# Seven products instead of eight in the second MLP product, with weight sums made in HBM

## The chip, the cores and the metric

The kernel runs on one core of a Trainium2 chip. The core has a matrix engine (TensorE, in the profile PE, with its weight loads as PEld), a vector engine (VectorE, DVE), a scalar engine (ScalarE, ACT), a general engine (GpSimd, POOL) and a queue that only issues transfers and waits (SyncE, SP). Each works through a queue of its own in order; they wait for each other by semaphores. Transfers are issued from SP, ACT or POOL and carried out by 16 DMA engines. The metric is the device time of one execution in microseconds.

## What is computed

One layer of a hybrid decoder on 512 tokens of 1024 channels, all in float32. What matters here is its last part, a squared-ReLU MLP with 4096 hidden channels:

```
x = x + mixed @ w_out
h = rms_norm(x, norm_mlp)
x = x + square(relu(h @ w_ff1)) @ w_ff2
out = rms_norm(x, norm_final)
```

Ahead of it come a causal pooling mixer and a sparse-attention mixer (projections of the normed input, a small MLP that compresses keys and values, rotary embedding, two softmax branches), merged by sigmoid gates. `w_ff1` is 1024 x 4096 and `w_ff2` 4096 x 1024, each 16 MB.

## The kernel before

Every matrix product of float32 numbers is made of three: each operand is split in a high part (a copy in the format that TensorE takes, by ScalarE) and a low part (the rest, by VectorE), and high x high, high x low and low x high are summed in PSUM. So each weight tile of 512 KB (128 x 1024 float32) is loaded to a raw tile, split into a pair of tiles, and then used. `emit_load` issues the loads in the order of a list `LD` on SP as raw tiles come free; `emit_prep_half` splits, in the order of a list `WL`; `use` hands out the split pair. `ahead()` is called between matmuls and prepares a few weights beyond the one in use.

The stages, with their times in the profile of before:

- 0 to 175 us: the input is normed and turned, and all projections with the pooling mixer and the compression run (`P1`, one weight tile of 512 KB after the other, each about 5.6 us of TensorE). Each of the key and query projections goes through `rope`, which copies PSUM out on ACT (L512) and swaps halves by four small DMAs on SP.
- to 395 us: attention, in 96 slots, with the remaining projections filled in between.
- to 476 us: the projection of the attention (`pn`), the output projection (`wo`), the residual sum, the second norm, and its transposition into quarters.
- to 777 us and to the end: the MLP in four chunks of 1024 hidden channels.

In the first MLP product each chunk is two groups of 512 hidden channels, and each group is a product of a 2 x 2 block matrix of weights (four quarters of 512 x 256) with a 2 x 2 block matrix of activations. It is done by seven block products instead of eight (Strassen's algorithm in Winograd's form). The seven are called A11, A12, A22, S1, S2, S3 and S4: the first three use a quarter of the weights as it is, the others use sums. VectorE makes the weight sums in place in the raw tiles (L231 to L238): S1 = 21 + 22, S3 = 11 - 21, S2 = S1 - 11, S4 = 12 - S2. Each block product is 24 matmuls with 256 columns (8 places x 3 products of parts), L1241, accumulated in a bank of PSUM; `Group.main` and `Group.last` combine the banks (L1285 to L1304), and `act` applies relu and square and splits the result into the two tiles `aT`. The second product of a chunk is plain: `tm3` runs 192 matmuls with 512 columns (L320) into eight banks and `add_x` (L1150) adds them to the residual, in both halves of the output channels. Between the two `drain_side()` completes what VectorE and ScalarE still have to do.

Eight raw tiles serve the MLP: four of the ring of the earlier stages and four cut from `oT`, the attention's output, once it is used up. Three pairs of split tiles go round.

The code is written in one order, with generators (`side`) that interleave the side work. The framework then sets the order of each engine's queue by its own planner, which may move an instruction ahead of others that stand before it in the text when its operands are ready and its engine has room in the plan. Transfers issued by SP and ACT are given eight semaphores in turn, and a transfer waits until the one before it on its semaphore has landed.

Of the kernel before, what the change touches and what calls it, by code (L numbers as in the profile page):

```python
# [62 lines left out]
def trunk(ctx: ExitStack, tc: tile.TileContext, A, out):  # L63
# [28 lines left out]
    def add_w(key, ap):  # L92
        WL.append((key, len(LD)))
        LD.append((ap, None))
# [40 lines left out]
    GROUPS = {}  # L135
# [3 lines left out]
    def add_group(c, g):  # L139

        c0 = 1024 * c + 512 * g
        GROUPS[c, g] = {"raw": {}, "at": {}}
        for q in ("11", "21", "22", "12"):
            r0, o = 512 * (int(q[1]) - 1), c0 + 256 * (int(q[0]) - 1)
            GROUPS[c, g]["at"][q] = len(LD)
            LD.append(([(w_f1[r0:r0 + 512, o:o + 256].rearrange("(k p) c -> p k c", p=128), 0)], (c, g, q)))

    for c in range(4):
        for g in range(2):
            add_group(c, g)  # L150
        if c == 0:
            order = [(g, o) for os in FIRST[:1] for o in os for g in range(2)]
            order += [(g, o) for os in FIRST[1:] for g in range(2) for o in os]
        else:
            order = [(g, o) for g in range(2) for o in IN_TURN]
        for g, o in order:
            WL.append((f"{o}{c}{g}", (c, g, o)))
        for h in range(2):
            for i in range(4):
                add_rows(f"f2{c}{h}{i}", w_f2, 1024 * c + 256 * i, 512 * h)  # L160
# [3 lines left out]
    st = {"load": 0, "prep": 0, "use": 0, "kept": 0}  # L164
    spare, slots_hl = [], []

    def emit_load():
# [4 lines left out]
        segs, quarter = LD[i]  # L172
# [3 lines left out]
        if quarter is None and not strassen_on() or st["kept"] < RAW:  # L176
            st["kept"] += strassen_on()
# [9 lines left out]
        if quarter is None:  # L187
            raws[i] = (t, a, b)
        else:
            GROUPS[quarter[:2]]["raw"][quarter[2]] = t  # L190
        return True

    def strassen_on():

        return st["load"] >= GROUPS[0, 0]["at"]["11"]

    def give_back(*tiles):
        spare.extend(tiles)
        while spare and strassen_on() and emit_load():
            pass  # L200

# [3 lines left out]
    def slot_of(i):  # L205

        if not isinstance(WL[i][1], int) or st["kept"]:
            n = len(slots_hl)
            if n < 2:
                slots_hl.append([wp.tile([128, 1024], FR, tag=f"w{e}", bufs=2, name=f"w{e}{i}") for e in "hl"])  # L210
            else:
                slots_hl.append(slots_hl.pop(0))
            return slots_hl[-1]
        return [wp.tile([128, 1024], FR, tag=f"w{e}", bufs=2, name=f"w{e}{i}") for e in "hl"]

    def group_steps(i):

        c, g, o = WL[i][1]
        G = GROUPS[c, g]
        while len(G["raw"]) < 4:  # L220
            assert emit_load()
        r = G["raw"]
        sm = GBf[:, 1024 + 1024 * g:2048 + 1024 * g]
        src = {"A11": r["11"], "A12": r["12"], "A22": r["22"], "S1": sm, "S2": r["11"], "S3": r["21"], "S4": r["12"]}[o]
        h, l = slot_of(i)
        ACT.activation(h, src, AF.Copy)
        yield
        DVE.tensor_tensor(l, src, h.bitcast(F32), op=ALU.subtract)
        if o == "A11":
            yield  # L230
            DVE.tensor_tensor(sm, r["21"], r["22"], op=ALU.add)  # L231
            yield
            DVE.tensor_tensor(r["21"], r["11"], r["21"], op=ALU.subtract)
            yield
            DVE.tensor_tensor(r["11"], sm, r["11"], op=ALU.subtract)
# [3 lines left out]
        G["done"] = G.get("done", "") + o  # L239
        dead = {"S3": "21", "A22": "22", "S4": "12"}.get(o)  # L240
        if o in ("A12", "S2") and "A12" in G["done"] and "S2" in G["done"]:
            dead = "11"
        hls[i] = tuple(x.rearrange("p (a b) -> p a b", a=4) for x in (h, l))
        if dead:
            give_back(r[dead])

    def emit_prep_half():
# [4 lines left out]
        if not isinstance(WL[i][1], int):  # L252
# [33 lines left out]
        if st["load"] > RAW + GROUPS[0, 0]["at"]["11"]:  # L286
# [114 lines left out]
    op = ctx.enter_context(pool("op"))  # L401
# [160 lines left out]
    with ExitStack() as c1:  # L562
# [222 lines left out]
    with ExitStack() as c2:  # L785
# [240 lines left out]
        for i in range(n + LAG + PLAG):  # L1026
# [18 lines left out]
            if 0 <= i - 1 < n:  # L1045
                weight(i - 1)
            if 0 <= t < n:
# [26 lines left out]
    give_back(*(oTf[:, 1024 * i:1024 * i + 1024] for i in range(4)))  # L1074
# [3 lines left out]
    X1 = [p3.tile([128, D], F32, name=f"x1_{t}") for t in range(NT)]  # L1078
    gB = p3.tile([128, D], F32, name="gB1")
# [3 lines left out]
    nc.sync.dma_start(gB, bcast(A["norm_mlp"][0], D))  # L1083
# [11 lines left out]
    def tm3(key, half, aT, post):  # L1095

        ps = [bank() for _ in range(NT)]
        for i in range(4):
            wH, wL = use(f"{key}{half}{i}")
            for t in range(NT):  # L1100
                sl = slice(128 * t, 128 * t + 128)
                prods = []
                for k in range(2):
                    prods += split_products(aT[0][:, 2 * i + k, sl], aT[1][:, 2 * i + k, sl], wH[:, k, :], wL[:, k, :])
# [6 lines left out]
    def tm3_resident(key, half, aT, post, parts=None):  # L1111
# [4 lines left out]
        for t in range(NT):  # L1116
            sl = slice(128 * t, 128 * t + 128)
            n = 256 if parts and t == NT - 1 else 512
            for c in range(0, 512, n):
                ps = bank()[:, 0:n]  # L1120
                prods = []
                for k in range(8):
                    wH, wL = ws[k // 2]
                    prods += split_products(aT[0][:, k, sl], aT[1][:, k, sl], wH[:, k % 2, c:c + n],
                                            wL[:, k % 2, c:c + n])
# [21 lines left out]
    XB = {b: [quarter(f, i) for f in Rf] for i, b in enumerate(("11", "21", "22", "T1"))}  # L1147

# [17 lines left out]
    with ExitStack() as c3:  # L1166
        q3 = c3.enter_context(pool("q3"))
        mT = (q3.tile([128, 8, S], FR, name="mH"), q3.tile([128, 8, S], FR, name="mL"))
        W1 = (q3.tile([128, 8, S], FR, name="W1H"), q3.tile([128, 8, S], FR, name="W1L"))
        keep([f"wo1{i}" for i in range(4)], W1)  # L1170
        ACT.activation(tick, GB[:, 7, 0:1], AF.Sqrt)
# [15 lines left out]
        tm3("wo", 0, mT, post0)  # L1187

        def to_fm(t):
# [21 lines left out]
            for o, d, x, y in (("T1", XT, XQ["12"], XQ["11"]), ("T3", XQ["12"], XQ["22"], XQ["12"]),  # L1211
                               ("T2", XQ["11"], XQ["22"], XT), ("T4", XQ["21"], XQ["21"], XQ["11"])):
                DVE.tensor_tensor(d[:, :, sl], x[:, :, sl], y[:, :, sl], op=ALU.subtract)
# [12 lines left out]
        tm3_resident("wo", 1, mT, post1)  # L1226
# [3 lines left out]
    slots_hl.insert(0, [a4.tile([128, 1024], FR, name=f"w3{e}") for e in "hl"])  # L1230
# [4 lines left out]
    def product(ps, key, x, first):  # L1235

        w, n = use(key), 0
        for f in range(2):
            for k in range(4):
                for u, v in ((0, 0), (0, 1), (1, 0)):  # L1240
                    PE.matmul(ps[:, 256 * f:256 * f + 256], w[u][:, k, 128 * f:128 * f + 128], XB[x][v][:, k, :],  # L1241
                              start=first and n == 0, stop=n == 23, skip_group_check=True)
# [4 lines left out]

    class Group:


        def __init__(self, c, g, aT):
            self.c, self.g, self.aT = c, g, aT
            self.s = pair(GBf, 6 + g)
            self.u2, self.u3, self.c21 = pair(MAf, 6 + g), pair(MAf, g), pair(MAf, 2 + g)
            self.ps, self.done = {}, set()

        def pe(self, o):
            key = f"{o}{self.c}{self.g}"
# [136 lines left out]
```

## Time and profile before

| | |
|---|---|
| time, median of 3 runs | 829.54 us (826.65 to 830.17) |
| the profiled execution | 829.27 us |
| its span, first to last instruction | 827.5 us |
| mean granted TensorE clock | 0.994 |
| PE / PEld busy | 801.9 us (97%) / 695.0 us (84%) |
| DVE / ACT / POOL busy | 569.8 us (69%) / 459.8 us (56%) / 166.2 us (20%) |
| moved by DMA | 78.36 MB, mean 95 GB/s |
| issue to landing of a 512 KB weight load (median) | 3.4 to 4.1 us |

A row of a group names line, engine, operation, what is written and read, shapes and count, then busy time, mean time of one in ns, and the idle time of the engine ahead of these instructions with what ended it. A row of the chain gives start, duration and what ran. A row of the stretches gives from and to, length, and for each of PE, PEld, DVE, ACT and POOL its busy time and count, then the granted clock, the busy share of the 16 DMA engines and GB/s. Busy times of PE overlap because matmuls are pipelined, so the pace of matmuls is best read as length of a stretch by count.

### The profile page before, as it was taken

How to read it: one execution, taken by the hardware profiler on the slowest of the kernel's cores; microseconds unless marked ns; L12 is line 12 of the kernel's file. 1: busy time of each engine (PE TensorE's matmuls, PEld its weight loads, DVE VectorE, ACT ScalarE, POOL GpSimd, SP SyncE). 2: the span in 40 equal slices, each digit the busy share in tenths (PEclk: the TensorE clock that was granted, in tenths of full speed). 3: DMA queues.
4: the chain of work that ended last, by engine and by line, in shares of the span. 5: the costliest groups of instructions: out<-in, count | busy, mean ns of one | idle time of the engine just before them, and what ended most of it. 6: DMA issues, size and time to landing. Idle time of an engine off the chain costs nothing.

```text
span 827.5 us, 12810 instructions
## 1 busy us (share of the span) xinstructions
PE 801.9 (97%) x4649; PEld 695.0 (84%) x4649; DVE 569.8 (69%) x1155; ACT 459.8 (56%) x945; POOL 166.2 (20%) x235
## 2 busy tenths in 40 slices
PE   7999999999998999999999989999999999999997
PEld 4889878887887888888787879889988899889986
DVE  7797744537978888887674788646864586458813
ACT  6566443337868888898333584622761376227711
POOL 6000000027765756652223000000000000000000
PEclk9999999999999999999999999999999999999999
DMA  9363632331030101115425004431353035313202
GB/s 304 96 178 114 183 90 89 103 96 44 14 90 27 40 26 40 47 58 178 153 77 178 1 26 162 147 99 30 116 161 100 28 102 159 97 51 103 78 0 103
DMA packets 83289, 78.36 MB, mean 95 GB/s; under 512 B 3573, under 2 KB 69657, under 8 KB 83226
## 3 DMA queue, kind: packets, MB, share of 16 engines
q1 hardware_dynamic: 82938, 76.75, 30.2%
q8 instruction: 37, 0.61, 0.3%
q10 hardware_dynamic: 288, 0.79, 0.3%
q14 instruction: 26, 0.21, 0.1%
HBM read 72.81 MB, written 2.10 MB: 91 GB/s over the span
## 4 chain that ended last, share of the span: by engine, by line
PE 80%; DVE 8%; ACT 4%; POOL 2%; issue 2%; DMA 2%; SPq 0%; POOLq 0%; ACTq 0%; DVEq 0%
PE psB L320 27%; PE psF L320 20%; PE psB L1241 18%; PE psO L1003 3%; PE psT L969 3%; PE psS L908 2%; PE psV L320 2%; DVE P L930 2%; DVE PT L984 1%; DMA raw<-w_out 1%; PE psF L374 1%; PE psC L608 1%; POOL P L953 1%; DVE x L457 1%; POOL wl L279 1%
## 5 line engine op out<-in xcount | busy, mean ns | idle before, releaser
L320 PE MATMUL psF<-R,wh 128*128 128x512 f32 x512 | 166.3, 404 | 0.2 <-ACT MA L766 0.2
L277 ACT ACTIVATE wh<-raw 128x512 fp32r<-128x512 f32 (+1 forms) x116 | 70.1, 620 | 101.8 <-PE psF L320 35.6
L320 PEld LDWEIGHTS psF<-R,wh 128*128 128x128 f32 x512 | 92.4, 189 | 17.8 <-ACT MA L766 0.5
L320 PE MATMUL psF<-R,wl 128*128 128x512 f32 x256 | 102.0, 398 | 0.8 <-DVE wl L279 0.8
L279 DVE TENSOR_TENSOR wl<-raw,wh 128x512 fp32r<-128x512 f32 (+1 forms) x92 | 65.4, 721 | 51.4 <-ACT wh L277 51.0
L953 POOL TENSOR_SCALAR P<-P,sm,GT 128x128 f32<-128x128 f32 (+3 forms) x128 | 83.1, 657 | 56.6 <-DVE sm L950 39.3
L320 PE MATMUL psB<-wh,aT 128*128 128x512 f32 x288 | 92.1, 395 | 0.0
L940 ACT ACTIVATE P<-P,sm 128x128 f32<-128x128 f32 (+3 forms) x128 | 71.1, 558 | 14.7 <-DVE sm L930 14.0
L1363 POOL TENSOR_TENSOR MA<-x,gB 128x512 f32<-128x512 f32 x1 | 1.3, 1287 | 350.7 <-DVE sq L1156 350.7
L1241 PE MATMUL psB<-R,wh 128*128 128x256 f32 x352 | 65.4, 286 | 2.3 <-ACT R L1214 2.1
L320 PEld LDWEIGHTS psB<-wh,aT 128*128 128x128 f32 x288 | 54.1, 188 | 12.8
L930 DVE CUSTOM_DVE_ANT_0 P<-psS,cst 128x128 f32<-128x128 f32 (+3 forms) x128 | 59.7, 484 | 5.2 <-PE psT L969 3.8
L279 POOL TENSOR_TENSOR wl<-raw,wh 128x512 fp32r<-128x512 f32 x28 | 38.7, 1387 | 106.0 <-ACT wh L277 103.6
L984 DVE TENSOR_TENSOR PT<-psT,PT 128x512 fp32r<-128x512 f32 (+2 forms) x96 | 56.6, 594 | 4.5 <-ACT PT L980 3.4
L320 PEld LDWEIGHTS psF<-R,wl 128*128 128x128 f32 x256 | 48.3, 189 | 11.8 <-DVE wl L279 0.9
L1241 PEld LDWEIGHTS psB<-R,wh 128*128 128x128 f32 x352 | 55.4, 192 | 3.0 <-ACT R L1214 2.3
L320 PE MATMUL psB<-wl,aT 128*128 128x512 f32 x144 | 56.9, 395 | 0.0
L980 ACT ACTIVATE PT<-psT 128x512 fp32r<-128x512 f32 (+2 forms) x96 | 49.2, 520 | 11.7 <-PE psT L969 10.9
L969 PE MATMUL psT<-ident,P 128*128 128x128 f32 x320 | 51.3, 275 | 3.4 <-POOL P L953 3.0
L969 PEld LDWEIGHTS psT<-ident,P 128*128 128x128 f32 x320 | 39.8, 141 | 13.8 <-POOL P L953 5.4
L320 PE MATMUL psB<-w3h,aT 128*128 128x512 f32 x160 | 51.0, 390 | 0.0
L1241 PE MATMUL psB<-R,wl 128*128 128x256 f32 x176 | 50.0, 284 | 0.0
(293 smaller groups left out, 1957.2 us busy)
## 6 DMA issues: line engine op xcount, KB each, us to landing
raw<-w_in SPq DMA_DIRECT2D x32, 512.0 KB, 3.8
oT<-w_ff SPq DMA_DIRECT2D x32, 512.0 KB, 3.9
raw<-w_ff SPq DMA_DIRECT2D x32, 512.0 KB, 3.6
raw<-w_proj_nsa SPq DMA_DIRECT2D x8, 512.0 KB, 3.8
raw<-w_out SPq DMA_DIRECT2D x8, 512.0 KB, 3.6
x<-x SPq DMA_DIRECT2D x7, 512.0 KB, 6.7
rs<-rx SPq DMA_DIRECT2D x40, 64.0 KB, 2.0
raw<-w_ck SPq DMA_DIRECT2D x4, 512.0 KB, 7.1
```

The costliest lines, as they stand in the source:

```text
L277: ACT.activation(h[:, sl], t[:, sl], AF.Copy)
L279: eng.tensor_tensor(l[:, sl], t[:, sl], h[:, sl].bitcast(F32), op=ALU.subtract)
L320: PE.matmul(ps, a, b, start=first and j == 0, stop=last and j == n - 1, skip_group_check=True)
L908: PE.matmul(ps[:, 0:n], q, rhs, start=a, stop=not a, skip_group_check=True)
L930: DVE.tensor_tensor_reduce(out=P[:, o:o + n].rearrange("p (a c) -> p a c", c=128), in0=s, in1=m, scale=1.0, scalar=3e38, op0=ALU.add, op1= ...
L940: last_exp[:] = [ACT.activation(c, c, AF.Exp, bias=sm[:, 0, e:e + 1], scale=-1.0, accum_out=sm[:, 1, e:e + 1])]
L953: POOL.tensor_scalar(P[:, o:o + n], P[:, o:o + n], sm[:, 2, e:e + 1], GT[:, qb, c + e:c + e + 1], op0=ALU.mult, op1=ALU.mult)
L969: PE.transpose(pt[:, 128 * j:128 * j + 128], P[:, 128 * j:128 * j + 128], ident)
L980: ACT.activation(dH, src, AF.Copy)
L984: DVE.tensor_tensor(dL, src, dH.bitcast(F32), op=ALU.subtract)
L1003: PE.matmul(ps[:, qb % 2, :, :], VV[:, k, b, g, :], t[:, j, :, :], start=False, stop=last and j == len(kbs) - 1 and t is tL, skip_group_ch ...
L1241: PE.matmul(ps[:, 256 * f:256 * f + 256], w[u][:, k, 128 * f:128 * f + 128], XB[x][v][:, k, :], start=first and n == 0, stop=n == 23, skip ...
```

## The change

The second product of chunks 0, 1 and 2 (`C_FF2 = 3`) also goes by seven products. The hidden activations of a chunk are now kept as four quarters (`YF`, in float32) and seven split operands (`YB`): 11, 21, 22 and the sums T1, T2, T3, T4, which `Hidden.sums` makes on VectorE. `Out` runs the seven products for each half of the output channels; the activations are the fixed operand and the weights move, 256 columns at a time, and `take` adds the banks into the residual `XX` and a helper `U`, which `fold` adds in at the end of the third chunk. The two halves alternate in the order `OUT_TURN`. The signs of some sums change: S3 is now 11 + 21 and S2 is S1 + 11, with the activations' sums to match. Chunk 3's second product stays plain.

The weight sums S1, S2 and S3 of each group, of both layers, are no longer made by VectorE. `make_sum` makes them in HBM: a plain copy of a quarter, issued by ACT, into a new HBM tensor, and then an accumulating DMA, issued by POOL, that adds another quarter (S1 = 21 + 22, S3 = 11 + 21, S2 = S1 + 11 with S1 copied first). There are 8 groups in the first layer and 6 in the second, so 42 sums. `make_sum()` is called in every second step of the projections, in every fourth slot of the attention, and in the `pn` steps, with what is left right behind them; each call issues the accumulation of the sum begun by the call before, and the copy of the next. S4 is still made by VectorE, from the raw tiles of S2 and A12, one of which is held until then (`held`).

In the built program the planner has placed the 42 copies among the first 178 entries of ACT's queue, the last of them just ahead of the evacuation of the fifth rope projection (L512 of before); all 42 accumulating DMAs stand in POOL's queue ahead of its first work for the attention.

Each sum is then loaded like any other weight tile, so a chunk loads 12 tiles for each layer instead of 8. `oT` is given up after the attention; five raw tiles serve the MLP. The tile for the gain vectors is loaded twice at other places, and the third pair of split tiles is made earlier.

```diff
-    IN_TURN = ("A11", "S2", "S3", "S1", "A12", "A22", "S4")
+    C_FF2 = 3
+    IN_TURN = ("A11", "S3", "S1", "S2", "A12", "A22", "S4")
+    OUT_TURN = ("A11", "A11", "S1", "S1", "A12", "A12", "S2", "S4", "S2", "S4", "S3", "S3", "A22", "A22")
+    dp = ctx.enter_context(tc.tile_pool(name="sums", bufs=1, space=bass.MemoryType.DRAM))
+    jobs = []
...
+    def add_group(layer, c, g):
+        q = quarters(layer, c, g)
+        of = {"A" + k: v for k, v in q.items()}
+        for o in ("S1", "S3", "S2"):
+            of[o] = dp.tile([128, 4, 256], F32, name=f"{o}_{layer}{c}{g}")
+        jobs.append((of["S1"], q["21"], q["22"]))
+        jobs.append((of["S3"], q["11"], q["21"]))
+        jobs.append((of["S2"], of["S1"], q["11"]))
+        return of
...
+    def make_sum():
+        if st["sums"] <= len(jobs):
+            if st["sums"]:
+                to, _, q = jobs[st["sums"] - 1]
+                POOL.dma_start(to, q, accum_op=ALU.add)
+            if st["sums"] < len(jobs):
+                to, q, _ = jobs[st["sums"]]
+                ACT.dma_start(to, q)
+            st["sums"] += 1
...
     def group_steps(i):
...
-        if o == "A11":
-            yield
-            DVE.tensor_tensor(sm, r["21"], r["22"], op=ALU.add)
-            yield
-            DVE.tensor_tensor(r["21"], r["11"], r["21"], op=ALU.subtract)
-            yield
-            DVE.tensor_tensor(r["11"], sm, r["11"], op=ALU.subtract)
-        elif o == "A12":
-            yield
-            DVE.tensor_tensor(r["12"], r["12"], r["11"], op=ALU.subtract)
...
+        to = SUM_OF.get(key)
+        if to is None:
+            give_back(t)
+        elif to not in held:
+            held[to] = t
+        else:
+            yield
+            DVE.tensor_tensor(t, t, held[to], op=ALU.add)
+            give_back(held[to])
+            held[to] = t
...
-        for k in P1[2:]:
+        for n, k in enumerate(P1[2:]):
             i = int(k[-1]) if k[-1].isdigit() else None
+            if n % 2:
+                make_sum()
...
+            if i % 4 == 2:
+                make_sum()
...
-    give_back(*(oTf[:, 1024 * i:1024 * i + 1024] for i in range(4)))
+    e2.close()
...
+    slots_hl.insert(0, [p4.tile([128, 1024], FR, name=f"w3{e}") for e in "hl"])
+    give_back(p4.tile([128, 1024], F32, name="raw5"))
...
+            make_sum()
             fm3(f"pn{j}", post, OT)
+        while st["sums"] <= len(jobs):
+            make_sum()
...
+    class Hidden:
+        def sums(self, f):
+            f11, f12, f21, f22 = (halves(YF[b], f) for b in ("11", "12", "21", "22"))
...
+            DVE.tensor_tensor(f11, f11, f12, op=ALU.subtract)
+            yield
+            yield from self.split("T1", f, f11)
...
+    class Out:
+        X = {"A11": ("a", "11"), "S1": ("d", "T1"), "A12": ("a", "21"), "S2": ("b", "T2"), "S4": ("d", "22"),
+             "S3": ("c", "T3"), "A22": ("c", "T4")}
+        def pe(self, o):
...
+            def mm(out, w, f, k, u, v, **kw):
+                PE.matmul(out, YB[y][u][:, k, 128 * f:128 * f + 128], w[v][:, k, :], **kw)
...
+            product(self.ps[name], f"{o}2{self.c}{self.h}", o not in self.AFTER, mm)
+            side.append(self.take(o, self.ps[name]))
...
     for c in range(4):
-        aT = [a4.tile([128, 8, S], FR, tag=f"a{e}", bufs=1, name="aT") for e in range(2)]
-        gs = [Group(c, g, aT) for g in range(2)]
+        Y = Hidden(c >= C_FF2)
+        gs = [Group(c, g, Y) for g in range(2)]
...
-        drain_side()
-        if c < 3:
-            for h in range(2):
-                tm3(f"f2{c}", h, aT, lambda t, ps, h=h: add_x(t, h, ps))
+        if c < C_FF2:
+            outs = [Out(c, h, Y) for h in range(2)]
+            seen = {}
+            for o in OUT_TURN:
+                h = seen.get(o, 0)
+                seen[o] = h + 1
+                outs[h].pe(o)
+            if c == C_FF2 - 1:
+                for x in outs:
+                    side.append(x.fold())
```

More of the change, by code (lines that the diff above doesn't have):

```diff
@@ new lines, in trunk @@
+        add_turn(1, c, of, turn)
+        if c < C_FF2:
+            of = [add_group(2, c, g) for g in range(2)]
+            seen = {}
+            turn = []
+            for o in OUT_TURN:
+                g = seen.get(o, 0)
+                seen[o] = g + 1
+                turn.append((g, o))
+            add_turn(2, c, of, turn)
+        else:
+            for h in range(2):
+                for i in range(4):
+                    add_rows(f"f2{c}{h}{i}", w_f2, 1024 * c + 256 * i, 512 * h)
@@ L161, in trunk @@
     dest = {}
     raws, hls = {}, {}
-    st = {"load": 0, "prep": 0, "use": 0, "kept": 0}
+    st = {"load": 0, "prep": 0, "use": 0, "kept": 0, "pairs": 0, "sums": 0}
     spare, slots_hl = [], []
+    held = {}
     def emit_load():
@@ L1304, in last @@
             DVE.tensor_tensor(to, self.ps[name], self.u2, op=ALU.add)
[L1305 to L1314 removed]
+            yield from self.Y.act(to, self.g, f, th)
@@ new lines, in halves, with __init__, of, split @@
+    def halves(x, f):
+        return x[:, 2 * f:2 * f + 2, :]
+    class Hidden:
+        def __init__(self, plain):
+            self.plain = plain
+            self.here = set()
+            if not plain:
+                for f in range(2):
+                    side.append(self.sums(f))
+        def of(self, b):
+            return YB["T1" if b == "12" else b]
+        def split(self, b, f, src):
+            hi, lo = (halves(x, f) for x in self.of(b))
+            ACT.activation(hi, src, AF.Copy)
@@ L1315, in act @@
             yield
             yield
-            DVE.tensor_tensor(lo, r, hi.bitcast(F32), op=ALU.subtract)
+            DVE.tensor_tensor(lo, src, hi.bitcast(F32), op=ALU.subtract)
+            self.here.add((b, f))
+        def act(self, src, g, f, th):
+            yield
+            b = f"{g + 1}{th + 1}"
+            r = halves(YF[b], f)
+            ACT.activation(r, src.rearrange("p (f t) -> p f t", f=2), AF.Relu, scale=-1.0 if f else 1.0)
+            ACT.activation(r, r, AF.Square)
+            if b != "12" or self.plain:
+                yield from self.split(b, f, r)
+            self.here.add((b, f))
```

249 lines of the change are left out of this document (146 added, 103 removed).

## The prediction

> **What bounds the kernel now.** I read the page first, then the chain of waits, then stretches of time.
>
> ```profile
> span 827.5 us, 12810 instructions
> PE 801.9 (97%) x4649; PEld 695.0 (84%) x4649; DVE 569.8 (69%) x1155; ACT 459.8 (56%) x945; POOL 166.2 (20%) x235
> q1 hardware_dynamic: 82938, 76.75, 30.2%
> ```
>
> TensorE is busy 97% of the span. What it is given to do, and whether the others feed it in time, sets the end. The profiled execution took 829.27 us (span 827.5 and 1.8 around it), 0.03% below the median of 829.54; my sums are made against 829.3. Some 0.5%, 4.1 us, is about what a measurement of this kernel can tell from no change.
>
> The MLP, as the chain that ended last has it (start, duration, what):
>
> ```profile
> 523.95 44.33 PE psB L320 x192
> 568.28 39.95 PE psB L1241 x336
> 608.23 44.43 PE psB L320 x192
> 652.66 39.95 PE psB L1241 x336
> 692.61 44.37 PE psB L320 x192
> 736.98 39.91 PE psB L1241 x336
> 776.89 44.67 PE psB L320 x216
> ```
>
> The chain never leaves TensorE here. L320 is the plain second product: 192 matmuls of 512 columns, 0.231 us each. L1241 is the first product by seven products: 336 of 256 columns, 0.119 us each. The seven products of a chunk are 4.4 us cheaper than the plain form of the same size.
>
> The other view that matters is that of stretches (busy time of PE, PEld, DVE, ACT, POOL, each with a count; then clock, DMA share, GB/s):
>
> ```profile
> 0.00:20.00 20.00, 13.92 (x57) 9.63 (x58) 14.21 (x22) 12.00 (x22) 12.49 (x27) 1.00 0.98 308
> 14.00:16.00 2.00, 2.00 (x13) 2.00 (x11) 1.36 (x2) 1.92 (x7) 2.00 (x3) 1.00 1.06 409
> 4.00:140.00 136.00, 132.03 (x680) 110.18 (x679) 95.27 (x182) 72.61 (x138) 13.95 (x26) 1.00 0.53 153
> 500.00:524.00 24.00, 24.00 (x203) 23.98 (x202) 19.73 (x26) 15.72 (x24) 0.00 (x0) 1.00 0.52 177
> 568.00:608.00 40.00, 40.00 (x338) 39.96 (x337) 30.94 (x35) 26.46 (x38) 0.00 (x0) 1.00 0.37 118
> 608.00:652.50 44.50, 44.50 (x194) 36.16 (x194) 22.70 (x29) 12.28 (x20) 0.00 (x0) 1.00 0.28 84
> ```
>
> Three things are to be seen. In the first 20 us the 16 DMA engines are full (share 0.98) at 308 GB/s, so that is what saturation looks like here; the best 2 us reach 409. From 4 to 140 us the projections run, TensorE is busy 132 of 136 us, and the DMA engines are already taken 0.53 of the time by 20.8 MB (153 GB/s x 136 us): 72 us used, 64 us free. The rows of 1 KB that the MLP's quarters have move at 177/0.52 = 340 GB/s, 1.54 us for 512 KB (0.524 MB) of all 16 engines.
>
> **The change, part by part.** *The second product, three chunks.* Per chunk 2 halves x 7 products x 24 = 336 matmuls of 256 columns take the place of 192 of 512. At the pace of the L1241 rows that is 39.94 us for 44.38. Gain 3 x 4.44 = 13.3 us. This is the whole benefit on TensorE; the first product keeps its 336 matmuls.
>
> *The work that must hide beside it.* Rows of the groups in the three full chunk pairs before:
>
> ```profile
> L228 DVE TENSOR_TENSOR wl<-raw,wh 128x1024 fp32r<-128x1024 f32 x12 | 14.7, 1226 | 14.9 <-ACT wh L226 14.9
> L1150 DVE TENSOR_TENSOR x<-psB,x 128x512 f32<-128x512 f32 x24 | 16.3, 688 | 8.1 <-PE psB L320 8.1
> L226 ACT ACTIVATE wh<-raw 128x1024 fp32r<-128x1024 f32 x12 | 12.7, 1055 | 29.8 <-PE psB L320 28.2 <-DVE raw L235 1.6
> L1311 ACT ACTIVATE r<-r 128x512 f32<-128x512 f32 x25 | 15.7, 629 | 0.6
> raw<-w_ff SPq DMA_DIRECT2D x32, 512.0 KB, 3.6
> ```
>
> VectorE per chunk after: 28 low parts of weights and 4 sums for S4 at 1.226 us (39.2 us), and at 0.688 us 10 combinations of the first product, 14 low parts and 8 sums of the hidden activations, 14 additions out of PSUM (46, 31.6 us): 70.8 of 79.9 us. Before it was 30.9 + 22.7 = 53.6 of 84.4. ScalarE: 28 x 1.055 + 32 x 0.629 = 49.7 us. Both fit, VectorE with 9 us to spare, so I cost them at nothing; were VectorE late, PSUM banks and weight pairs would come late, and I allow up to 8 us over the three chunks for that. The three weight sums of a group that VectorE made leave it; that relief is inside the 70.8.
>
> *Loads.* 24 of 512 KB per chunk instead of 16, on SP: 12.6 MB in 79.9 us, 157 GB/s, against 308 at saturation: hidden. There are five raw tiles instead of eight, and while two are held for S4 sums, two or three circulate: 3.6 + 1.06 + 1.23 = 5.9 us for two, 2.95 us a product against 39.94/14 = 2.85. That is short by 0.1 us for a few products a chunk, and covered by the third pair of split tiles: nothing.
>
> *Norm tiles.* The last gain vector is loaded behind the third chunk instead of early; it has the 44.67 us of the last plain product to land: nothing. The attention loop keeps its instructions. Around 475 to 500 us the first chunk's order is the same.
>
> *The sums in HBM.* 14 groups (8 of the first layer, 6 of the second) x 3 = 42 sums: 42 plain copies HBM to HBM issued by ACT, and 42 accumulating DMAs issued by POOL, each 512 KB. The text of the kernel spreads them from the projections through the attention. In the built program they stand elsewhere: all 42 copies are among ACT's first 178 entries, the last just ahead of the copy out of PSUM for the fifth rope; and all 42 accumulating DMAs stand ahead of POOL's first attention work. That place in the trace of before, with the first and the price of an issue on ACT:
>
> ```profile
> 0.73 0.38 ACTq L425 DMA_DIRECT2D x<-x  x1
> 30.68 0.60 ACT L512 ACTIVATE rx<-psF 128x512 f32<-128x512 f32 x1
> 140.59 0.58 ACT L512 ACTIVATE rx<-psF 128x512 f32<-128x512 f32 x1
> ```
>
> So 7 copies stand ahead of ACT's work at 30.7 us and all 42 ahead of that at 140.6 us. Issuing costs ACT 42 x 0.38 = 16 us in a stretch in which it is busy 72.6 of 136: hidden. The waits are what is not hidden. The copy of S2 reads S1 and so waits, on ACT's queue, until the accumulation into S1 has landed; POOL's accumulation waits until its copy has landed; and SP's and ACT's DMAs share eight semaphores in turn, so each waits for an earlier one. The last S2 copy waits for the 39th accumulation. Hence ACT cannot go past the place that it now reaches at 140.6 us until 39 copies and 39 accumulations are through the DMA engines. Behind the waiting copy on ACT stand the high parts of every projection weight (L277 of before) and the copies out of PSUM, for which TensorE and VectorE wait; TensorE has two or three weights in hand and then stands. POOL's own work behind its waits (small copies) is not needed sooner.
>
> The trace has neither a copy from HBM to HBM nor an accumulation, so I bound them. Below: both cost what a load of 1 KB rows costs, 1.6 us of all engines. Above: every byte read and every byte written counts, 3.2 us for a copy (one read, one write) and 4.8 for an accumulation (two reads, one write). A gain is excluded, as nothing is removed from this stretch. I take the middle for the copy, 2.4, and for the accumulation 3.2, the load's price twice, since it must read two operands of 512 KB. Then 39 x 5.6 = 218 us are wanted where 64 are free: +154 us. The ends: 39 x 3.2 = 125, +61; 39 x 8.0 = 312, +248.
>
> On copies inside HBM the Trainium skill ("DMA: Bandwidth & Descriptors", section "Latency and other measured facts") gives 207 to 214 GB/s per direction as the full rate; by that a copy would be 2.5 us (an estimate), the stretch +158 and the time 974. No row here shows such a copy.
>
> Sum: 829.3 - 13.3 + 154 = 970 us; ends 877 and 1064.
>
> **Rivals.** *The sums are nearly hidden, and it gets faster.* 20.8 MB of loads and 78 x 0.524 = 40.9 MB of sums are 61.7 MB. If an accumulation costs no more than its 512 KB and the engines run beyond the best stretch, the projections grow by less than the 13.3 us gained. The point is 61.7 MB/149.3 us = 413 GB/s. For it: 409 in the best 2 us. Against it: 308 over the 20 us in which the queue was never empty, and one place where every load would have to be at its best for 150 us. At 409 the stretch grows by 15 us and the time is 831 (no change); at 450 it grows by 1 and the time is 817.
> The Trainium skill's page "DMA: Bandwidth & Descriptors" (section "Where 436 GB/s comes from") puts the ceiling at 435 GB/s; at that rate the stretch would grow by 6 us and the time be 822. The trace's 409 agrees with the ceiling and its 308 says that it is not held.
>
> *POOL is the bound.* If POOL itself needs more than (136 + 154)/39 = 7.4 us to issue one accumulation, POOL and not the DMA engines sets the stretch; at 10 us each, 390 us, +254, and 1070 us. No instruction of POOL that issues a DMA is in the trace; the nearest, SP's and ACT's, take 0.4 us, which speaks against it.
> The Trainium skill's page "SBUF — State Buffer" (the box on the DVE blocks DMA trap) says that POOL's descriptors wait while VectorE holds the port they share; no row here shows that.
>
> *VectorE becomes the bound of the MLP.* 70.8 us of 79.9 speak against it. Each us that it lacked would cost 3 in all; with the sums hidden it would give 816 to 824.
>
> **How the numbers follow.** Forecast (the DMA engines saturate in the projections, 877 to 1064 us): 0.77. POOL as the bound: 0.10. No change, at 409 GB/s: 0.04. Faster, at more: 0.09. Faster by over 0.5%: 0.09; within: 0.04; slower: 0.77 + 0.10 = 0.87. The time is the forecast's, 970. The range leaves out the 0.13 of no change and faster, and 0.07 of the highest: 860 (the low end with 1.54 us for each transfer is 872; 12 less for sums still in flight when ACT goes on) to 1080. It holds one sign only.
>
> **What would show it.** After the change the fifth rope's copy out of PSUM on ACT, at 140.6 us now, should come near 295 us. In the slices before it DMA should read 0.9 or more and PE 5 tenths; PE's waits should name the high part of the projection weights, and ACT's the DMAs into S1. POOL's queue should show accumulating DMAs in the projections and none in the attention. The attention should keep its length. In the MLP three pieces of the chain of 44.4 us should become 40.0, with VectorE near nine tenths. The prediction is wrong if DMA stays under 0.9 there and ACT's waits are short, that is, if accumulations are cheap; or if the MLP loses on VectorE what it gains on TensorE.

## The result, and the profile after

| | before | after |
|---|---|---|
| time, median of 4 runs | 829.29 us (826.65 to 830.17) | 915.11 us (912.81 to 916.4) |
| ratio, 95% interval | | 1.1038 (1.1003 to 1.1072) |
| the profiled execution, its span | 829.27, 827.5 us | 916.4, 914.6 us |
| mean granted TensorE clock | 0.994 | 0.942 |

The change costs 86 us. From the page of the kernel after: busy times, the slices of TensorE, of its clock and of the DMA engines, and the queues (q0 is POOL's with the accumulations, q10 ACT's with the copies, q1 SP's).

```profile
span 914.6 us, 13951 instructions
PE 809.3 (88%) x5081; PEld 720.8 (79%) x5081; DVE 600.9 (66%) x1195; ACT 482.9 (53%) x959; POOL 212.1 (23%) x277
...
PE   5849594367799999999999999999999999999997
...
PEclk8979797678789999999999999999999999999999
DMA  9999999999933020201105333063654355364602
...
q1 hardware_dynamic: 87738, 91.44, 32.2%
q0 software_dynamic: 22176, 22.02, 15.4%
q10 hardware_dynamic: 15520, 22.81, 6.9%
```

A slice is 22.9 us. For the first eleven, to about 250 us, the DMA engines are full, and just there TensorE has its holes and its clock falls. From 300 us on nothing looks worse than before. The stretches of the kernel after, columns as before:

```profile
4.00:238.70 234.70, 154.48 (x696) 126.81 (x695) 91.50 (x182) 72.41 (x139) 58.59 (x66) 0.80 1.13 267
160.00:180.00 20.00, 4.86 (x21) 3.50 (x20) 2.02 (x5) 0.94 (x3) 3.53 (x4) 0.67 1.15 234
```

The same projections that took 4 to 140 us take until 238.7 us, with a DMA share of 1.13; between 160 and 180 us TensorE works 4.9 of 20 us. The end of that stretch on ACT, the copy out of PSUM for the fifth rope, in order of time:

```profile
238.68 0.60 ACT L549 ACTIVATE rx<-psF 128x512 f32<-128x512 f32 x1 [5.54 <-DMA S<-w_ff]
```

It stood at 140.59 us: +98.1. What was waited for in the first 280 us (total, times, longest):

```profile
POOL S L238 <- DMA S<-w_ff: 86.7, 23, 10.2
POOL S L238 <- DMA S<-S: 80.4, 13, 11.3
...
ACT MA L805 <- DMA S<-w_ff: 37.6, 3, 15.8
...
PE psF L356 <- ACT MA L805: 31.3, 4, 12.2
...
PE psC L645 <- ACT wkt L313: 12.9, 1, 12.9
...
PE psV L356 <- ACT wh L313: 11.5, 1, 11.5
...
PE psF L356 <- ACT wh L313: 10.4, 1, 10.4
```

TensorE waits for high parts of weights and for copies out of PSUM by ACT, and ACT (and POOL) wait for transfers into the sums. The groups and transfers themselves (for the transfers: size, median us from issue to landing):

```profile
L238 POOL DMA_DIRECT2D S<-w_ff x42 | 49.3, 1184 | 175.7 <-DMA S<-w_ff 86.7
S<-w_ff POOLq DMA_DIRECT2D x42, 512.0 KB, 10.5
raw<-w_in SPq DMA_DIRECT2D x32, 512.0 KB, 7.7
S<-w_ff ACTq DMA_DIRECT2D x28, 512.0 KB, 9.9
S<-S ACTq DMA_DIRECT2D x14, 512.0 KB, 6.4
```

An accumulation takes POOL 1.18 us to issue and lands 10.5 us later; a projection weight of 512 KB lands after 7.7 us, about 3.8 before. Behind it, the MLP in the chain of the kernel after:

```profile
498.00 30.73 PE psB L356 x131
...
637.20 25.79 PE psB L1438 x214
662.98 34.11 PE psB L1322 x287
...
743.45 34.12 PE psB L1322 x287
...
823.90 39.92 PE psB L1322 x336
863.81 44.67 PE psB L356 x216
```

The first line is the projection behind the attention, at 395.46 us before: +102.5, as the end of the projections (175.4 to 278.0, +102.5 too), so the attention kept its length. The first product of the chunks 1, 2 and 3 starts at 663.0, 743.5 and 823.9 instead of 568.3, 652.7 and 737.0: +94.7, +90.8, +86.9. A pair of products takes 80.5 us instead of 84.4. So the change lost 102.5 us in the projections and won 15.6 behind the attention.

### The profile page after: what moved, and what is told of

Same layout as the page of the kernel before. It is cut to its first block, busy times and chain, and to the rows that moved or that the text cites. A ratio compares the mean times of both kernels' runs of the same rounds, so it can differ in the third digit from the quotient of the medians.

```text
span 914.6 us, 13951 instructions
## 1 busy us (share of the span) xinstructions
PE 809.3 (88%) x5081; PEld 720.8 (79%) x5081; DVE 600.9 (66%) x1195; ACT 482.9 (53%) x959; POOL 212.1 (23%) x277
## 3 DMA queue, kind: packets, MB, share of 16 engines
q0 software_dynamic: 22176, 22.02, 15.4%
## 4 chain that ended last, share of the span: by engine, by line
PE 49%; DVE 11%; ACT 5%; issue 3%; POOL 2%; DMA 1%; SPq 0%; ACTq 0%; POOLq 0%; DVEq 0%
PE psB L1322 14%; PE psB L356 11%; PE psB L1438 8%; PE psF L356 8%; PE psO L1042 2%; PE psT L1008 2%; PE psS L947 2%; DVE P L969 1%; DMA raw<-w_out 1%; DVE wl L270 1%; ACT P L979 1%; DVE PT L1023 1%; POOL P L992 1%; POOL wl L315 1%; ACT PT L1019 1%
## 5 line engine op out<-in xcount | busy, mean ns | idle before, releaser
L356 PE MATMUL psF<-R,wh 128*128 128x512 f32 x512 | 174.3, 420 | 39.7 <-ACT MA L805 29.3
L356 PEld LDWEIGHTS psF<-R,wh 128*128 128x128 f32 x512 | 97.4, 199 | 59.0 <-ACT MA L805 29.9
L268 ACT ACTIVATE wh<-raw 128x1024 fp32r<-128x1024 f32 x66 | 69.7, 1057 | 74.9 <-PE psB L1438 32.5
L356 PE MATMUL psF<-R,wl 128*128 128x512 f32 x256 | 105.5, 412 | 0.8 <-DVE wl L315 0.7
L315 DVE TENSOR_TENSOR wl<-raw,wh 128x512 fp32r<-128x512 f32 (+1 forms) x78 | 55.8, 732 | 57.2 <-ACT wh L313 57.1
L270 DVE TENSOR_TENSOR wl<-raw,wh 128x1024 fp32r<-128x1024 f32 x66 | 80.6, 1222 | 19.4 <-ACT wh L268 19.1
L238 POOL DMA_DIRECT2D S<-w_ff x42 | 49.3, 1184 | 175.7 <-DMA S<-w_ff 86.7
L313 ACT ACTIVATE wh<-raw 128x512 fp32r<-128x512 f32 (+1 forms) x102 | 60.3, 618 | 50.2 <-issue 16.2
L356 PEld LDWEIGHTS psF<-R,wl 128*128 128x128 f32 x256 | 50.7, 198 | 13.4 <-DVE wl L315 1.9
L268 ACT ACTIVATE w3h<-raw 128x1024 fp32r<-128x1024 f32 x32 | 33.8, 1056 | 37.7 <-PE psB L1438 15.8
## 6 DMA issues: line engine op xcount, KB each, us to landing
S<-w_ff POOLq DMA_DIRECT2D x42, 512.0 KB, 10.5
```

Source lines behind the costliest of these rows:

```text
L268: ACT.activation(h, t, AF.Copy)
L270: DVE.tensor_tensor(l, t, h.bitcast(F32), op=ALU.subtract)
L313: ACT.activation(h[:, sl], t[:, sl], AF.Copy)
L315: eng.tensor_tensor(l[:, sl], t[:, sl], h[:, sl].bitcast(F32), op=ALU.subtract)
L356: PE.matmul(ps, a, b, start=first and j == 0, stop=last and j == n - 1, skip_group_check=True)
```

## The experiments

The theory: the loss is engine time of DMA, brought together by the planner in the projections. The rivals: the waits that S2's copy puts on ACT; POOL's issuing; VectorE or the loads in the MLP. The last ones were free to show themselves in the first run. The numbers in brackets behind a median are its lowest and highest run; kernels run once are given with one time, and a few us mean little there.

**Without the sums.** S1, S3 and S2 are loaded from plain quarters and nothing is summed in HBM; the work on the engines is that of the kernel after.

```diff
-        for o in ("S1", "S3", "S2"): ... jobs.append(...)
+        of.update(S1=q["21"], S3=q["11"], S2=q["22"])
```

> The MLP part of the change alone. Leaves out all 42 sums in HBM; S1, S2 and S3 are loaded from plain quarters of the weights instead, so the weights of three products in seven are not the sums. Number of loads, splits and matmuls is that of the changed kernel. Both theories (saturated DMA engines, and waits in the queues) blame the sums, so both expect the projections as before the change (fifth rope's copy out of PSUM on ACT at 140 us) and the MLP of the changed kernel: 915.1 - 102.5 = 812.6, that is 808 to 818 us. Above 825 would mean that the move to seven products costs something that neither names.

814.62 us (813.19 to 815.12), ratio 0.982 [0.9794, 0.9846]. Chain of this kernel:

```profile
395.08 30.72 PE psB L351 x131
...
560.66 34.12 PE psB L1317 x287
...
761.49 44.67 PE psB L351 x216
```

The projection behind the attention starts at 395.08 us as before the change (395.46). The second product by seven, the extra loads and VectorE's new work are worth 14.9 us together, and the sums in HBM lost all the rest: 915.1 - 814.6 = 100.5 us. VectorE and the loads fall as rivals.

**S2 without its wait on ACT.** S2's copy starts from a quarter, so that no copy waits for an accumulation (S2 then holds 21 + 11).

```diff
-        jobs.append((of["S2"], of["S1"], q["11"]))
+        jobs.append((of["S2"], q["21"], q["11"]))
```

> The same 84 transfers of the same size, but the copy of S2 starts from quarter 21 instead of from S1, so ACT no longer waits for the accumulation into S1 (this leaves quarter 22 out of S2). Saturated DMA engines: the amount is the same, so the fifth rope's copy stays at 225 to 250 us and the time at 900 to 925. Waits on ACT's queue as the cause: ACT's waits for the sums, some 80 us of the first 240, go, and the time falls below 860.

895.31 us, 5 us below the range that I gave for saturation. The fifth rope stands at 219.7 us, the projection behind the attention at 476.7, 81.6 later than without sums. So some 20 of the 102 us go with the waits of S2's copies, by this one run. With them gone the engines are still full up to the fifth rope:

```profile
4.00:219.70 215.70, 155.31 (x705) 127.12 (x703) 92.19 (x182) 73.28 (x139) 56.98 (x64) 0.87 1.16 276
```

**A plain copy in place of the accumulation.** POOL issues 42 plain copies of the same size (the sums are left out).

```diff
-                POOL.dma_start(to, q, accum_op=ALU.add)
+                POOL.dma_start(to, q)
```

> POOL's 42 transfers are plain copies of the same size to the same place instead of accumulations (S1, S2 and S3 are then single quarters). Same queues, same waits. Saturated DMA engines, with 3.35 us of all engines for an accumulation (141 us of POOL's queue by 42) and 1.44 for a copy: (72 + 39 x 2.88)/1.13 = 163 us of transfers ahead of the fifth rope's copy, which comes near 167 us, and a time near 840 (830 to 855). If it is POOL's issuing that costs, whatever the transfer does: 905 to 920. If it is the waits in the queues: not under 870.

865.98 us. The queues of this kernel's page, and the stretch to its fifth rope:

```profile
q10 hardware_dynamic: 15520, 22.81, 7.7%
q0 software_dynamic: 6048, 22.02, 7.1%
...
4.00:189.50 185.50, 146.21 (x685) 121.05 (x684) 91.55 (x182) 72.40 (x139) 39.64 (x65) 0.89 1.00 334
```

POOL issues as often as in the kernel after and the loss halves (+52 us at the projection behind the attention, with a share of 1.00 to the fifth rope). An issue is also shorter here, 0.71 us instead of 1.18. That issuing isn't the bound shows in the kernel after itself: its 42 issues take POOL 49.3 us, and POOL stood idle for 175.7 us ahead of them (the L238 row). The prices of a transfer of 512 KB in time of all 16 engines follow from the queues: the copy on POOL 7.1% x 864.2/42 = 1.46 us, the accumulation (kernel after) 15.4% x 914.6/42 = 3.35 us, the copy on ACT there (6.9% - 0.3% for ACT's other transfers, as without sums) x 914.6/42 = 1.44 us. These are sums of packet times; in the full stretches of these runs they come to shares of 1.00 to 1.16, so packet times overlap on an engine, and a price is no time on the clock. An accumulation costs 2.3 copies; it also goes as 22176/42 = 528 packets where POOL's plain copy goes as 144. The time is 11 us above the range that I gave for saturation: with the prices now known, 84 copies at 1.46 to 1.52 us are 125 us where 64 are free, +61; the fifth rope moved by 48 (141.4 to 189.5 us). The direction was right and the size missed, and by this run alone the waits as a part of the loss were not excluded; the run before bounds those of S2's copies. The forecast also divided by the share of 1.13, and this stretch ran at 1.00.

**Copies alone.** The 42 accumulations are left out, the copies stay.

```diff
-                POOL.dma_start(to, q, accum_op=ALU.add)
+                pass
```

> POOL's 42 accumulations are left out, the 42 copies stay where they are (S1, S2 and S3 are then single quarters). Saturated DMA engines, reckoned by the bytes that are read: 20.8 MB of loads and 22 MB of copies in 136 us are 315 GB/s, which the engines can just do, so the projections grow by 0 to 12 us over the kernel without sums: 815 to 830 us. Waits on ACT's queue as the cause: the copy of S2 still waits for the one into S1, and the time stays above 840.

822.21 us, 8 us above the kernel without sums: 42 copies at 1.44 to 1.54 us (the latter from the queues of this kernel) are 60 to 65 us of engine time, about the 64 us that were free there. So a load as large as the free time costs little; at which load the loss begins was not run.

**The sums of the first layer alone.** The 18 sums of the second layer are left out.

```diff
+        if layer == 2:
+            of.update(S1=q["21"], S3=q["11"], S2=q["22"])
+            return of
```

> Only the 24 sums of the first layer are made in HBM, drawn forward by the planner as before; S1, S2 and S3 of the second layer are loaded from plain quarters instead of sums. Saturated DMA engines: 20.8 MB of loads and 24 x 3 x 0.524 MB read for sums are 58.5 MB, at 350 GB/s 167 us, so the projections grow by some 30 us over the kernel without sums: 845 (835 to 855). If each sum costs its waits, whatever the load on the engines: 24/42 of 102 us, 58, and 873.

866.06 us: a miss, above the range for saturation and nearer the figure for a loss in proportion. The copies out of PSUM for the third and the fourth rope on ACT, and the stretch to the third:

```profile
134.91 0.60 ACT L552 ACTIVATE rx<-psF 128x512 f32<-128x512 f32 x1 [8.21 <-PE psF L359]
169.99 0.58 ACT L552 ACTIVATE rx<-psF 128x512 f32<-128x512 f32 x1
...
4.00:134.90 130.90, 96.30 (x486) 82.20 (x484) 66.35 (x130) 51.94 (x100) 33.76 (x43) 0.88 1.13 278
```

Without sums the third stands at 90.5 us and the fourth at 117.8, the fifth at 141.4. So 44 of the 52 us are lost by the third rope, and from the fourth on (+52.2, +52.2) nothing more. I had set the sums against the free time up to the fifth rope; 24 sums are planned ahead of the third and fourth, and the free time behind that place never helps them. The cover is that of the place, not of the stage.

**The order of the text kept.** Each copy and accumulation is held at its place in the program text: 15 accumulations issued in the projections, 25 in the attention, 2 behind it.

```diff
-                POOL.dma_start(to, q, accum_op=ALU.add)
+                tc.keep_in_program_order(POOL.dma_start(to, q, accum_op=ALU.add))
...
-                ACT.dma_start(to, q)
+                tc.keep_in_program_order(ACT.dma_start(to, q))
```

> All sums are made as in the changed kernel, but each copy and each accumulation is kept behind what the text has ahead of it on its engine, so that the planner does not draw them forward: 15 in the projections from 30 us on, 25 in the attention, the rest behind it. Saturated DMA engines: in the projections 72 + 15 x 4.8 = 144 us of transfers for 175 us, in the attention 68 + 25 x 4.8 = 188 for 295, so neither saturates for long: 815 to 840 us. Waits in the queues as the cause: ACT and POOL wait in the attention as they did in the projections, and the time stays above 860.

839.05 us (836.93 to 840.13), ratio 1.0114 [1.0088, 1.0139]. This gives back 76 us without a byte less, so it is where the planner put them. It is still 24 us above the kernel without sums: the projection behind the attention is 26.9 us late. In its chain stand transfers:

```profile
105.02 6.85 DMA rs<-rx
...
283.90 7.95 DMA S<-w_ff
...
334.05 6.54 DMA rs<-rx
```

`rs<-rx` are the small transfers that swap halves for the rope; without sums the slowest of them landed after 4.0 us.

**An even spread.** By the trace 6 accumulations are issued in the projections, 18 in the attention up to 400 us (most of them behind its last rope), 6 from 400 to 460 us, where the projections behind it begin, and 12 later, nearly all beside the MLP, one in four block products; S2's copy stands behind the sums of both groups, so that it doesn't wait. All 42 sums are made.

```diff
-            if n % 2:
+            if n % 4 == 1 and n > 4:
...
-            if i % 4 == 2:
+            if i % 4 == 2 if i > 53 else i % 9 == 4:
...
+        st["products"] = st.get("products", 0) + 1
+        if st["products"] % 4 == 1:
+            make_sum()
```

> All 42 sums, spread over the kernel: 7 in the projections, 6 in the attention while projections with rope are still mixed in, 12 behind the last rope, 6 in the pn steps, the rest beside the MLP, one in four block products. Each is kept behind what the text has ahead of it, and the copy of S2 is begun four sums after S1 instead of two. Saturated DMA engines: 4.6 us of transfers about every 13 us saturate nothing, so at most 12 us are lost against the 814.6 without sums: 815 to 828 us, below the kernel before. Waits as the cause, at 102/42 = 2.4 us a sum wherever it stands: some 840 or more, as with e5.

> As e6, but the copies are issued by POOL too, ahead of the accumulation of the sum begun before, so that ACT neither issues nor waits for a transfer. Saturated DMA engines: the same amount at the same places, 815 to 830 us; POOL has 42 more issues of 1.16 us, in the attention some 17, which may cost a few us there. If ACT's waits are what is left of the loss, e7 comes out below e6 by more than 5 us.

The second has the copies issued by POOL too. 838.67 us (835.27 to 842.55), ratio 1.0097 [1.006, 1.0135], and 841.69 us (837.76 to 845.45), ratio 1.0147 [1.0106, 1.0187]. Both missed. Nothing is gained where ACT issues no copies. But the second kernel's accumulations also come earlier (the last is issued at 531.7 us, in the first at 632.3), so this pair does not change the issuer alone. Two stretches of the first:

```profile
400.00:440.00 40.00, 35.63 (x148) 27.55 (x147) 20.49 (x27) 15.55 (x28) 11.92 (x10) 0.96 1.06 278
560.00:640.00 80.00, 80.00 (x673) 79.95 (x674) 65.61 (x77) 45.46 (x60) 8.10 (x7) 1.00 0.90 244
```

In the MLP the engines are 0.9 busy and TensorE loses nothing. At 400 to 440 us, where the sums meet the loads of the next stage, the share is 1.06 and TensorE stands 4.4 of 40 us. The chain there:

```profile
410.88 11.56 DMA S<-w_ff
...
446.75 8.79 DMA raw<-w_out
...
521.66 9.72 DMA raw<-w_ff
```

The first of these is POOL, which stands in an accumulation until its copy has landed, with the low part of a weight behind it. So two causes were open: the place, or POOL's wait for its copy.

**Other places, and a longer lag.** No sum is begun in the first projections, among the ropes of the attention, or between the attention and the MLP; 10 are begun in the second half of the projections, 11 late in the attention, 21 beside the MLP. And each accumulation two calls behind its copy, not one. All sums are made here and in the next three.

```diff
-            if n % 4 == 1 and n > 4:
+            if n % 2 and n > 12:
...
-            if i % 4 == 2 if i > 53 else i % 9 == 4:
+            if i % 4 == 2 and 53 < i < 98:
...
-            make_sum()
             fm3(f"pn{j}", post, OT)
...
-        if st["products"] % 4 == 1:
+        if st["products"] % (4 if st["products"] < 29 else 3) == 0 and st["products"] > 7:
...
-                to, _, q = jobs[n - 1]
+                to, _, q = jobs[n - 2]
```

> All 42 sums made. None among the first projections, among the rope projections of the attention, or at the projections behind it; 10 in the second half of the projections, 11 late in the attention, 21 beside the first three MLP chunks from the eighth block product on, and each accumulation is issued two calls behind its copy instead of one, so that POOL does not wait for the copy. Theory 'the price is one of places: transfers that something waits for land late where the engines are crowded, and POOL's waiting accumulations hold up the low parts of weights': the 4 us at the first projections, 8 among the ropes and 16 at the entry of the projections behind the attention go; 814.6 us (no sums) plus 3 to 12: 818 to 827 us. Rival 'every sum has its price wherever it is (24 us over 42 sums, 0.57 us each)': 836 to 841 us as with the even spread.

> As e8_lag, with the copies issued by SP instead of ACT. Theory of places: SP's queue waits for raw tiles in the MLP, so copies come later there, but nothing on ACT or POOL is held up by them: within 4 us of e8_lag, 817 to 829 us. If ACT's 21 issues of 0.6 us beside the attention and the projections are what is left, 3 to 8 us below e8_lag. Rival 'price per sum': 836 to 841 us.

The second has SP issue the copies. 821.31 us (818.89 to 823.07), ratio 0.9909 [0.9882, 0.9935], and 819.91 us (817.15 to 821.53), ratio 0.99 [0.988, 0.9921]: both about 1% below the kernel before, and both intervals lie below 1. The accumulations come at the same times in both, and the copies' issuer makes no difference that these runs can tell. A price per sum wherever it is made falls. To tell place from lag, one of each alone:

```diff
 the even spread:
-                to, _, q = jobs[n - 1]
+                to, _, q = jobs[n - 2]
 the other places:
-                to, _, q = jobs[n - 2]
+                to, _, q = jobs[n - 1]
```

> The even spread with the second call of lag alone, the places as they were. If the waiting accumulations on POOL are the cause of what the even spread lost: 12 us go at the entry of the projections behind the attention and most of the rest, 818 to 826 us. If the places are the cause (transfers that land late where the engines are crowded): the share stays above 1 at 400 to 440 us and the loads there stay late, 833 to 841 us. Both in parts: 826 to 833 us.

> The places of e8_lag alone, with one call of lag as in the even spread. If the places are the cause: as e8_lag, 818 to 825 us. If the waits on POOL are the cause: 831 to 840 us. Both in parts: 825 to 831 us.

The lag alone: 839.97 us (838.68 to 844.1), ratio 1.0149 [1.0115, 1.0183]. The places alone: 818.83 us (816.99 to 820.5), ratio 0.9877 [0.9856, 0.9898], the lowest median with all sums made, though its runs overlap with those of the two kernels before. The places decide, and the lag shows no gain at either set of places. With the lag alone the projection behind the attention does start earlier (409.25 us for 425.48), but the longest load of `w_out` in the chain still takes 6.7 us (8.8 in the even spread, 4.4 without sums), and 12 of these 16 us are lost again by the first product of chunk 1 (584.77 for 588.66 us): the wait on POOL was replaced by the next late thing. A stretch of that kernel, then two stretches of the kernel with the other places (where the projection behind the attention starts at 397.45 us) and two lines of its chain:

```profile
400.00:440.00 40.00, 37.65 (x164) 29.65 (x163) 22.99 (x28) 15.59 (x28) 15.12 (x12) 1.00 1.07 280
```

```profile
400.00:440.00 40.00, 40.00 (x171) 32.21 (x171) 24.67 (x27) 11.75 (x20) 9.72 (x7) 0.99 0.38 130
560.00:680.00 120.00, 119.63 (x1005) 119.42 (x1004) 95.55 (x110) 67.27 (x88) 16.21 (x14) 1.00 1.03 276
...
564.63 39.95 PE psB L1327 x336
...
766.01 44.67 PE psB L361 x216
```

The engines are as full in the MLP (1.03) as they were between the stages (1.07), and there it costs TensorE 0.4 of 120 us. From the first product of chunk 1 to the last second product this kernel takes 201.4 us, with 16 accumulations beside it; without sums it is 200.8 us. The MLP's list of loads goes on ahead of the products, so a load that lands late is still early enough; between the stages the loads are needed when they land. That last sentence is read from the code and these rows; it was not tested by itself, nor was it run apart which of the places left empty carries how much. Against the kernel without sums 4.2 us remain (818.83 - 814.62), and the chains have nearly all of them ahead of chunk 1 (564.63 for 560.66 us).

## Why the prediction was right, and where its size was off

Forecast was a loss by DMA engines that saturate in the projections, 970 us, 860 to 1080. It was 915: the sign and the mechanism were right, the size was 55 us too high. Two terms were too dear, and the range was wide enough to take that.

- *The second product* (13.3 us): 14.9 measured without the sums. The chunk pairs give 3.9 us each, not 4.44, and the first chunk with the steps ahead of it 7.3, in part because TensorE's idle time there fell from 4.1 to 1.9 us; this extra I had not counted.
- *VectorE, ScalarE, loads, norm tiles at nothing:* right. A pair of products takes 80.5 us where 79.9 was worked out, and VectorE was busy 136 of the 161 us of two pairs (85%), so its 9 us to spare were enough and the allowance of 8 wasn't used.
- *The attention keeps its length:* right, +102.5 us at both ends.
- *The place:* right. The fifth rope came at 238.7 us, where 295 was forecast, behind waits of ACT for transfers into the sums; holding the order of the text gave back 76 us.
- *The price of a copy* is the term that was mis-sized: 2.4 us taken, 1.44 measured, below the low end of 1.6. The accumulation was taken as 3.2 and measured 3.35. So 39 sums are 39 x 4.79 = 187 us of engine time instead of 218: +123 instead of +154.
- *What a full stretch holds* was the other: I counted a share of 1.00 as full, and the stretch ran at 1.13 (the page's share had read 1.06 in the best 2 us of before, which I quoted and did not use). The loads' 72 us and the sums' 187 are 259; over 1.13 they are 229 us, and 4 + 229 = 233 us is near the 238.7 that were measured. That only shows that the terms add up, since prices and share come from the same kernel. The 1.13 is no rule: the stretch with plain copies ran at 1.00, where my forecast by 1.13 missed, and the one with S2 freed at 1.16.
- *One wait in the sum:* I took the waits on ACT as only the way by which the engines' time shows. By the kernel with S2 freed, run once, some 20 of the 102 us go with the waits of S2's copies; the rest remains with them gone. How these 20 us divide between the waits and the fuller engines (1.16 for 1.13) was not measured.

The Trainium skill ("DMA: Bandwidth & Descriptors", section "Latency and other measured facts") has 207 to 214 GB/s for copies inside HBM, by which a copy would be 2.5 us (an estimate). The runs differ: 0.524 MB in 1.44 us of packet time are 364 GB/s, the stretch with plain copies moved 334 GB/s, loads and copies together, and the measurement decides. The same page's "Rules for kernel authors" says that an accumulating transfer reads its destination and writes it later; the 3.35 us for 1.46 of a plain copy on the same queue agree with more being moved.

The rivals: *nearly hidden* needed 413 GB/s over the stretch, and the engines held 267 with accumulations and 334 with copies in their place. *POOL as the bound* needed 7.4 us an issue; it was 1.18. *VectorE as the bound of the MLP* did not show (85% busy).

## What to carry to other kernels

Work moved to the DMA engines has a price in engine time per transfer and a place; set the first against the free engine time at the place where the built program has it, not against that of the stage or of the span. Transfers that nobody waits for cost next to nothing here beside the MLP, where the loads run well ahead of their use, though the engines were full; they cost 24 us where part of them ran beside small transfers and beside first loads of a stage that are used as they land. Try the first kind of place first. Where a planner orders the queues, look for where it put transfers without near deadlines: here that order alone made 76 of 100 us, and another choice of places turned +10% into -1.2%.

## What the runs showed of the hardware beyond that

- An accumulating transfer HBM to HBM of 512 KB takes 3.35 us of all 16 engines in the saturated kernel and 18.8% x 818.3/42 = 3.66 us where the sums are spread with the longer lag; a plain copy 1.44 to 1.54. These are packet times, as above. The page of the profile counts an accumulation's bytes like a copy's (22.02 MB for 42), so the GB/s of a stretch full of them look low (267 against 334) though the engines are busier.
- Issuing it takes POOL 1.18 us, a plain copy of the same size 0.71 us; ACT's copies take 0.5 to 0.7 us.
- In the stretches in which TensorE starved its granted clock fell to 0.67, and it was 0.80 over the whole stretch, against 1.00 before; and a matmul that at last has its operands also took longer: those of 512 columns in the projections had a mean of 430 ns for 397. The time that this adds to the whole was not measured by itself.
